# The first microseconds of an encoder step: unread bf16 products on TensorE, a norm's row factors by float32r products, and another order of weights and norms

## The chip, the cores and the metric

The kernel runs on one core of one Trainium2 chip. A core has five engines that work side by side, each with a queue of its own: TensorE (PE, matrix products into PSUM), VectorE (DVE), ScalarE (ACT), GpSimd (POOL) and SyncE (SP, which here only issues DMA transfers). An engine takes its instructions in order, and an instruction may wait on semaphores that other engines or transfers raise. The metric is the time of one execution in microseconds (us), as the median of several runs.

## The reference, cut to what matters

Two layers, each with three parts: a feed-forward block (FFN 1), a mixer with four branches, and a second feed-forward block (FFN 2). 384 frames of width 1024 go through them (256 of one new stream, 16 of each of 8 running streams). What the change touches is the very start: the first norm of FFN 1 and the first columns of its product.

```python
def rmsnorm(x, g):
    xf = x.astype(jnp.float32)
    xf = xf * lax.rsqrt(jnp.mean(jnp.square(xf), axis=-1, keepdims=True) + EPS)
    return (xf * g.astype(jnp.float32)).astype(x.dtype)

def swiglu_ffn(x, g_pre, g_post, w_gu, w_down):
    gate, up = jnp.split(rmsnorm(x, g_pre) @ w_gu, 2, axis=-1)
    return rmsnorm((jax.nn.silu(gate) * up) @ w_down, g_post)
```

## The kernel before

The 384 frames stand as three tiles of 128 frames (`x0`, `x1`, `x2`, in the code `self.x[t]`), frames on the partitions. All large products are made in float32r. Each operand is split in a high part (`wh`, `xh`: a copy cast to float32r, by ACT) and a low part (`wl`, `xl`: the rest, a subtraction by DVE), and a product is the sum of three: high by high, low by high, high by low (`mm3`).

Weights come in units of 512 KB, in the fixed order of `plan_units`. A unit is loaded by SP into one of four staging buffers (`st`), cast by ACT (`wh`) and subtracted by DVE (`wl`); only then is the staging buffer free, and SP loads the unit that stands four places later. The first four units are `ffn_gs` (here s0 to s3, called by number), 2 rows of 128 of the first 512 columns each; then `ffn_gp` and `ffn_dn` units follow.

Every norm of a tile goes through `chain`: ACT squares the two halves of the tile and sums them (`out` is a scratch tile `junk`, one buffer for all users; the sums go to `pre`), DVE adds a constant, POOL takes the power -1/2, DVE multiplies tile, factor and `gain` (SCALAR_TENSOR_TENSOR, two halves), PE transposes 4 blocks of each half (`acc<-ident,half`), ACT casts them to `xh` (two halves), DVE subtracts `xl` (two halves). `gain` is the row of 1024 norm factors on all 128 partitions. For the first norm it is made from one loaded row (`row`) by a product with a column of ones, in plain float32, and copied out of PSUM by DVE; later norms load it spread.

`ffn_head` then makes the first 512 columns for each frame tile in turn: 8 steps k of three products of 512 columns (`rot<-wh,xh`, `rot<-wl,xh`, `rot<-wh,xl`), two k per weight unit. So tile 0 needs s0 for k = 0 and 1, s1 for k = 2 and 3, s2 for k = 4 and 5, s3 for k = 6 and 7. After the three tiles `ffn_body` begins, with products of 384 columns from the `ffn_gp` units (`rot<-xh,wh` and so on).

The order in which work is written to the engines is made by a planner in Python. `self.now` is its clock; `tick` advances it by the estimated cost of each TensorE instruction, and pops queued steps (`spawn`, `yield`) that have come due, `pump` emits the next weight unit when the estimates of ACT and DVE leave room. A step with a due time (a number that is yielded, as in `chain(..., at)`) is not written before the planner's clock has reached it. So the due times of the three norms, 4000, 7000 and 10000, set where they stand among the weight casts. The estimates set the order only; on the chip each instruction starts when its engine and its semaphores let it.

The lines that matter: `run` holds the start (the row's products, the loads, the three `spawn(("xT", t), ...)`), `chain` the norms, `split_unit` the weights, `heads` the first products.

Of the kernel before, what the change touches and what calls it, by code (L numbers as in the profile page):

```python
# [8 lines left out]
F32 = mybir.dt.float32  # L9
F32R = mybir.dt.float32r  # L10
BF16 = mybir.dt.bfloat16
AF = mybir.ActivationFunctionType
ALU = mybir.AluOpType
# [3 lines left out]
P = 128  # L17
D = 1024
# [30 lines left out]
PE, ACT, DVE, POOL = "tensor", "scalar", "vector", "gpsimd"  # L49
# [50 lines left out]
class Core:  # L100
# [545 lines left out]
    def mixer_front(self, l, m, mf, ma, aT, yT):  # L646
# [201 lines left out]
        with pool("mixq") as mq:  # L848
# [48 lines left out]

            self.heads(keys, main, mid)
            run(conv(0))

            def latent_kv(t, pb):
# [98 lines left out]
            for j in range(4):  # L1000
# [6 lines left out]
                if j % 2:  # L1007
                    self.done(("uq", l, 1 + j // 2))
            run(conv(1))
            self.need(("lat",))  # L1010

# [101 lines left out]
        with pool("mixs") as ms:  # L1113
# [102 lines left out]
            for j in range(4):  # L1216
                o = self.bank()[:, :P]
                for i in range(2):
                    h = 2 * j + i
                    for k in range(2):  # L1220
                        mm(o[i * 64:(i + 1) * 64, :], lhsT=wuv[:, k, h * 64:(h + 1) * 64],
                           rhs=qa[:, k, :, h * S:(h + 1) * S], start=(k == 0), stop=(k == 1))
                self.spawn(("att",), attended(j, o), "acc")
        run(fillers)
        for f in self.idle:
            f()
# [90 lines left out]
    def run(self):  # L1317
        nc, tc, a = self.nc, self.tc, self.a
# [10 lines left out]
        with ExitStack() as es:  # L1329
# [21 lines left out]
            row = self.gains.tile([P, D], F32, tag="g", name="row")  # L1351
# [10 lines left out]

            gain = self.gains.tile([P, D], F32, tag="g", name="gain")
            es.enter_context(tc.manual_schedule(engines=ENGINES))
            one = self.half()[:, :P]
            nc.vector.memset(one[0:1], 1.0)
            for h in range(2):
                o = self.acc(2, h)
                nc.tensor.matmul(o, lhsT=one[0:1], rhs=row[0:1, h * 512:h * 512 + 512], start=True, stop=True)
                nc.vector.tensor_copy(gain[:, h * 512:h * 512 + 512], o)  # L1370
            load_x(1)
            self.arrival += 1456
            self.load_unit()
# [2 lines left out]
            self.load_unit()  # L1376
            self.load_unit()
            for t in range(NT):
                self.spawn(("xT", t), self.chain(t, None, None, gain, 4000 + 3000 * t))
            self.ffn_pool()  # L1380
            for l in range(self.depth):
                m = {}
# [153 lines left out]
```

## Time and profile before

| | us |
|---|---|
| median of 3 runs (1858.26 to 1858.51) | 1858.48 |
| the profiled execution | 1858.79 |
| its span, first to last instruction | 1857.0 |
| PE busy in the span | 1831.8 |

The profile is of one execution. Its span is 1.79 us shorter than the time of the same execution. PE is the engine to look at first: it is busy for 99% of the span. The start can be told apart by stretches: up to 8.51 us PE has only the row's products, from there to 32.88 us it makes the head of the first block, and at 32.88 us the first product of 384 columns begins.

### The profile page before, as it was taken

The numbers are of one execution on the slowest core, as the hardware profiler recorded it, in microseconds if no ns is written. First come the engines' busy times: TensorE is split into PE (matmuls) and PEld (weight loads), VectorE is DVE, ScalarE is ACT, GpSimd is POOL, SyncE is SP. The second block draws the span as 40 slices with busy tenths as digits, with TensorE's granted clock in tenths as the row PEclk, the third lists the DMA queues.
The fourth block names the chain that finished last, engine by engine and source line by source line (L and its number), as shares of the span: only waits on it lengthen the run. The fifth ranks groups of instructions, "written<-read, shape, count | busy, mean of one in ns | idle before, by whom it ended". The sixth has DMA issues, their size and how long they took to land.

```text
span 1857.0 us, 25073 instructions
## 1 busy us (share of the span) xinstructions
PE 1831.8 (99%) x10060; PEld 1704.4 (92%) x10060; DVE 952.6 (51%) x1466; ACT 699.7 (38%) x1156; POOL 47.7 (3%) x96
## 2 busy tenths in 40 slices
PE   8999999999999999999999999999999999999998
PEld 6999998889999889999989999988899998999997
DVE  5333347896544463333463333478864446533333
ACT  5333334444333443333343333445343335333332
POOL 0000001000000000000000000010000000000000
PEclk9999999999999999999999999999999999999999
DMA  7444443452343443344444434344523434443441
GB/s 252 137 125 125 125 146 94 142 178 83 114 137 124 146 159 125 125 126 126 134 137 126 128 130 129 117 102 139 173 73 127 142 123 136 148 127 126 133 125 46
DMA packets 98087, 241.88 MB, mean 130 GB/s; under 512 B 28977, under 2 KB 39985, under 8 KB 97970
## 3 DMA queue, kind: packets, MB, share of 16 engines
q1 hardware_dynamic: 97826, 240.21, 41.4%
q8 instruction: 79, 1.29, 0.3%
q14 instruction: 38, 0.31, 0.1%
q10 hardware_dynamic: 144, 0.07, 0.0%
HBM read 236.63 MB, written 3.31 MB: 129 GB/s over the span
## 4 chain that ended last, share of the span: by engine, by line
PE 93%; DVE 4%; ACT 1%; issue 1%; POOL 0%; DMA 0%; POOLq 0%; DVEq 0%; ACTq 0%
PE rot L74 59%; PE acc L74 34%; DVE yTb L74 1%; DVE wl L74 1%; DVE half L74 1%; ACT wh L74 0%; ACT junk L74 0%; DVE sv L74 0%; DVE yTd L74 0%; DVE qTp L74 0%; DVE qa L74 0%; DVE xl L74 0%; DMA st<-in_f 0%; POOL ln L74 0%; POOL kv L74 0%
## 5 line engine op out<-in xcount | busy, mean ns | idle before, releaser
L74 DVE TENSOR_TENSOR wl<-st,wh 128x1024 fp32r<-128x1024 f32 (+3 forms) x426 | 500.1, 1185 | 479.3 <-ACT wh L74 468.3
L74 ACT CAST wh<-st 128x1024 fp32r<-128x1024 f32 (+3 forms) x426 | 428.5, 1018 | 665.1 <-issue 366.3
L74 PE MATMUL rot<-xh,wh 128*128 128x384 f32 x1984 | 669.1, 337 | 0.7 <-ACT sg L74 0.7
L74 PE MATMUL rot<-xh,wl 128*128 128x384 f32 x1984 | 665.7, 336 | 0.6 <-DVE wl L74 0.6
L74 PE MATMUL rot<-xl,wh 128*128 128x384 f32 x1984 | 665.1, 335 | 0.0
L74 PEld LDWEIGHTS rot<-xh,wh 128*128 128x128 f32 x1984 | 372.5, 188 | 8.0 <-issue 3.2
L74 PEld LDWEIGHTS rot<-xh,wl 128*128 128x128 f32 x1984 | 372.6, 188 | 5.0 <-DVE wl L74 1.0
L74 PEld LDWEIGHTS rot<-xl,wh 128*128 128x128 f32 x1984 | 372.5, 188 | 0.3 <-issue 0.3
L74 PE MATMUL acc<-wl,hh 128*128 128x512 f32 x528 | 207.2, 392 | 0.0
L74 PE MATMUL acc<-wh,hl 128*128 128x512 f32 x528 | 207.1, 392 | 0.0
L74 PE MATMUL acc<-wh,hh 128*128 128x512 f32 x528 | 205.4, 389 | 0.0
L74 DVE TENSOR_TENSOR hf<-sg,rot 128x384 f32<-128x384 f32 x80 | 44.4, 555 | 146.0 <-PE rot L74 146.0
L74 PEld LDWEIGHTS acc<-wl,hh 128*128 128x128 f32 x528 | 99.1, 188 | 20.8
L74 PEld LDWEIGHTS acc<-wh,hl 128*128 128x128 f32 x528 | 99.1, 188 | 19.1
L74 PEld LDWEIGHTS acc<-wh,hh 128*128 128x128 f32 x528 | 99.2, 188 | 18.9
L74 ACT ACTIVATE half<-rot 128x384 f32<-128x384 f32 x58 | 28.5, 492 | 167.2 <-PE rot L74 167.2
L74 DVE SCALAR_TENSOR_TENSOR half<-half,acc 128x384 f32<-128x384 f32 x44 | 24.4, 554 | 124.1 <-PE acc L74 124.1
L74 DVE SCALAR_TENSOR_TENSOR yTb<-bs,cols,yTb 128x384 f32<-128x384 f32 x120 | 73.8, 615 | 2.1
L74 PE MATMUL rot<-wl,xh 128*128 128x512 f32 (+1 forms) x144 | 55.7, 387 | 1.6 <-DVE wl L74 1.6
L74 PE MATMUL rot<-wh,xh 128*128 128x512 f32 (+1 forms) x144 | 56.3, 391 | 0.0
L74 PE MATMUL acc<-ident,half 128*128 128x128 f32 x262 | 43.9, 283 | 6.7 <-DVE half L74 5.4
L74 POOL TENSOR_TENSOR post<-post,neghalf 128x1 f32<-128x1 f32 x18 | 12.2, 679 | 1440.2 <-DVE post L74 1440.0
(221 smaller groups left out, 1631.7 us busy)
## 6 DMA issues: line engine op xcount, KB each, us to landing
st<-ffn_gp SPq DMA_DIRECT2D x160, 512.0 KB, 3.5
st<-ffn_dn SPq DMA_DIRECT2D x88, 512.0 KB, 3.5
st<-in_g SPq DMA_DIRECT2D x64, 512.0 KB, 3.7
st<-in_f SPq DMA_DIRECT2D x24, 512.0 KB, 4.0
st<-ffn_gs SPq DMA_DIRECT2D x16, 512.0 KB, 4.8
st<-w_o SPq DMA_DIRECT2D x16, 512.0 KB, 4.2
st<-w_br SPq DMA_DIRECT2D x16, 384.0 KB, 3.1
st<-in_b SPq DMA_DIRECT2D x8, 512.0 KB, 4.9
```

What stands on the lines that cost most here:

```text
L74: r = f(*args, **kw)
```

## The change

Three things are done differently in `run`, before and at the first norm.

1. DVE fills the scratch tile `junk` (128 x 512, bf16) with ones, and PE multiplies it by itself 9 times into a PSUM tile that nobody reads (`idle(9)`); after the row's products it does so 11 times more (`idle(11)`). All 20 write the same PSUM buffer, `acc(1, 1)`.
2. The row is split: ACT makes a row of ones and the high part `rh` in float32r, DVE subtracts the low part `rl` (all three lie in parts of `xl` that are not in use yet), and each half of `gain` is the sum of two float32r products where it was one float32 product.
3. The planner is kept from popping work meanwhile (`self.busy`), its clock and its engine estimates are set to zero behind the products, the due times of the norms are 4000, 8200 and 12500, and `pump` is called once more.

```diff
-            one = self.half()[:, :P]
-            nc.vector.memset(one[0:1], 1.0)
+            some = self.junk(512)
+            nc.vector.memset(some, 1.0)
+            rh, rl = (self.xl[0:1, 3 * i:3 * i + 3, :].rearrange("p k t -> p (k t)")[:, :D] for i in range(2))
+            one = self.xl[0:1, 6, 0:P]
+            self.busy = True
+            def idle(n):
+                for _ in range(n):
+                    nc.tensor.matmul(self.acc(1, 1), lhsT=some[:, :P], rhs=some, start=True, stop=True)
+            idle(9)
+            nc.scalar.activation(one, self.ones[0:1], AF.Copy, scale=256.0)
+            nc.scalar.copy(rh, row[0:1])
+            nc.vector.tensor_tensor(rl, row[0:1], rh.bitcast(F32), op=ALU.subtract)
             for h in range(2):
+                sl = slice(h * 512, h * 512 + 512)
                 o = self.acc(2, h)
-                nc.tensor.matmul(o, lhsT=one[0:1], rhs=row[0:1, h * 512:h * 512 + 512], start=True, stop=True)
-                nc.vector.tensor_copy(gain[:, h * 512:h * 512 + 512], o)
+                nc.tensor.matmul(o, lhsT=one, rhs=rh[:, sl], start=True, stop=False)
+                nc.tensor.matmul(o, lhsT=one, rhs=rl[:, sl], start=False, stop=True)
+                nc.vector.tensor_copy(gain[:, sl], o)
+            idle(11)
+            self.now, self.busy = 0.0, False
+            self.free = {e: 0.0 for e in (ACT, DVE, POOL)}
...
-                self.spawn(("xT", t), self.chain(t, None, None, gain, 4000 + 3000 * t))
+                self.spawn(("xT", t), self.chain(t, None, None, gain, (4000, 8200, 12500)[t]))
+            self.pump()
```

What stands on the engines is shown at three places; words in brackets behind a row name the semaphores it waits for (an engine's name, or a transfer's DMAHW number). Behind the head, PE has the same rows in the same order before and after.

PE at the start of the program, before: the row's two products, the transposes of tile 0, the first products.

```order
L74 MATMUL acc<-row,half 128x512 [waits DMAHW1_49,DVE_49]
L74 MATMUL acc<-row,half 128x512
L74 MATMUL acc<-ident,half 128x128 [waits DMAHW0_49,DVE_49]
L74 MATMUL acc<-ident,half 128x128 x3
```

PE at the same place in the change; `junk` is the tile of ones, `xl` the split row. Of each run of unread products the first two and the last are shown.

```order
L74 LDWEIGHTS junk [waits DVE_49]
L74 MATMUL acc<-junk 128x512
L74 LDWEIGHTS junk
L74 MATMUL acc<-junk 128x512 [waits PE_49]
...
L74 MATMUL acc<-xl 128x512 [waits Activation_49]
L74 MATMUL acc<-xl 128x512 [waits DVE_49]
L74 MATMUL acc<-xl 128x512 x2
...
L74 MATMUL acc<-junk 128x512 [waits PE_49]
L74 MATMUL acc<-ident,half 128x128 [waits DMAHW0_49,DVE_49]
```

The 20 unread products stand ahead of the transposes of tile 0, and each of them but the first waits for PE's own semaphore, which is raised by the product that wrote the PSUM buffer before it.

ACT from the first norm on, before: squares of tile 0 (`x_98`), s0, squares of tile 1 (`x_99`), the casts of tile 0, s1, squares of tile 2 (`x_100`), s2.

```order
L74 ACTIVATE junk,pre<-x_98 128x512 [waits DMAHW2_49]
L74 ACTIVATE junk,pre<-x_98 128x512 [waits Activation_49]
L74 CAST wh<-st 128x1024 [waits DMAHW3_49]
L74 ACTIVATE junk,pre<-x_99 128x512 [waits DMAHW4_49,Activation_49]
L74 ACTIVATE junk,pre<-x_99 128x512 [waits Activation_49]
L74 CAST xh<-acc 128x4x128 [waits PE_49] x2
L74 CAST wh<-st 128x1024 [waits DMAHW5_49]
L74 ACTIVATE junk,pre<-x_100 128x512 [waits DMAHW6_49,Activation_49]
L74 ACTIVATE junk,pre<-x_100 128x512 [waits Activation_49]
L74 CAST wh<-st 128x1024 [waits DMAHW7_49]
```

ACT at the same place in the change.

```order
L74 ACTIVATE xl<-ones 1x128 [waits DVE_49]
L74 CAST xl<-row 1x1024 [waits DMAHW1_49]
L74 ACTIVATE junk,pre<-x_98 128x512 [waits DMAHW2_49,DVE_49,PE_49]
L74 ACTIVATE junk,pre<-x_98 128x512 [waits Activation_49]
L74 CAST wh<-st 128x1024 [waits DMAHW3_49]
L74 CAST xh<-acc 128x4x128 [waits PE_49] x2
L74 CAST wh<-st 128x1024 [waits DMAHW5_49]
L74 ACTIVATE junk,pre<-x_99 128x512 [waits DMAHW4_49,Activation_49]
L74 ACTIVATE junk,pre<-x_99 128x512 [waits Activation_49]
L74 CAST wh<-st 128x1024 [waits DMAHW7_49]
L74 CAST wh<-st 128x1024 [waits DMAHW0_49]
L74 ACTIVATE junk,pre<-x_100 128x512 [waits DMAHW6_49,Activation_49]
```

The first square has two more waits, DVE and PE: it writes the scratch tile that the unread products read. The squares of tile 1 have moved behind s1, and s2 and s3 ahead of the squares of tile 2.

DVE from tile 1's norm on, before.

```order
L74 TENSOR_SCALAR pre<-pre 128x1 [waits Activation_49]
L74 TENSOR_TENSOR xl<-acc,xh 128x4x128 [waits Activation_49]
L74 SCALAR_TENSOR_TENSOR half<-x_99,pre,gain 128x512 [waits DMAHW4_49,Pool_49]
L74 SCALAR_TENSOR_TENSOR half<-x_99,pre,gain 128x512
L74 TENSOR_TENSOR xl<-acc,xh 128x4x128 [waits Activation_49]
L74 TENSOR_TENSOR wl<-st,wh 128x1024 [waits DMAHW5_49,Activation_49]
```

DVE at the same place in the change.

```order
L74 TENSOR_TENSOR wl<-st,wh 128x1024 [waits DMAHW5_49,Activation_49]
L74 TENSOR_SCALAR pre<-pre 128x1 [waits Activation_49]
L74 SCALAR_TENSOR_TENSOR half<-x_99,pre,gain 128x512 [waits DMAHW4_49,Pool_49]
L74 SCALAR_TENSOR_TENSOR half<-x_99,pre,gain 128x512
L74 TENSOR_TENSOR wl<-st,wh 128x1024 [waits DMAHW7_49,Activation_49]
L74 TENSOR_TENSOR wl<-st,wh 128x1024 [waits DMAHW0_49,Activation_49]
```

The low part of s1 has moved ahead of tile 1's norm, and the low parts of s2 and s3 stand right behind it.

## Rows read from the trace of the kernel before

**Rows 1.** The page's first lines: span; busy time, share, instructions of PE.

```profile
span 1857.0 us, 25073 instructions
PE 1831.8 (99%) x10060; PEld 1704.4 (92%) x10060; DVE 952.6 (51%) x1466; ACT 699.7 (38%) x1156; POOL 47.7 (3%) x96
```

**Rows 2.** Stretches: from:to, length, busy per engine (instructions), granted clock, DMA share, GB/s.

```profile
0.00:8.51 8.51, 3.75 (x4) 1.16 (x5) 2.67 (x8) 4.62 (x9) 0.76 (x5) 1.00 0.76 272
8.51:14.25 5.74, 5.74 (x20) 4.54 (x20) 5.67 (x9) 4.78 (x10) 0.55 (x1) 1.00 1.01 394
14.25:32.88 18.63, 17.01 (x82) 13.79 (x82) 11.40 (x18) 9.11 (x16) 2.41 (x3) 1.00 0.69 218
32.88:140.00 107.12, 107.12 (x573) 101.14 (x571) 43.15 (x47) 36.67 (x48) 0.00 (x0) 1.00 0.44 142
```

**Rows 3.** Chain that ended last, its start: start, length, what (0 to 35 us).

```profile
2.44 3.76 PE acc L74 x4
...
6.83 0.21 DVE pre L74
...
8.51 1.98 PE acc L74 x8
...
10.52 0.03 ACT xh L74
...
18.05 1.23 DVE wl L74
...
19.32 0.97 PE rot L74 x3
20.29 0.44 PE acc L74 x4
```

**Rows 4.** Timeline, PE: start, length, operation, tiles, shapes, [idle before, releaser].

```profile
11.32 0.63 PE L74 MATMUL rot<-wh,xl 128*128 128x512 f32 x1
11.74 0.63 PE L74 MATMUL rot<-wh,xh 128*128 128x512 f32 x1
...
19.32 0.50 PE L74 MATMUL rot<-wl,xh 128*128 128x512 f32 x1 [1.62 <-DVE wl L74]
...
22.63 0.39 PE L74 MATMUL rot<-wh,xl 128*128 128x512 f32 x1
...
26.25 0.39 PE L74 MATMUL rot<-wh,xh 128*128 128x512 f32 x1
...
32.88 0.33 PE L74 MATMUL rot<-xh,wh 128*128 128x384 f32 x1
```

**Rows 5.** Timeline, DVE, ACT and POOL in the first norm.

```profile
0.86 0.17 DVE L74 MEMSET ones<- 128x128 f32 x1
0.99 0.17 DVE L74 MEMSET half<- 1x128 f32 x1
...
4.81 0.63 ACT L74 ACTIVATE junk<-x 128x512 bf16<-128x512 f32 x1 [2.38 <-DMA x<-x]
...
5.56 0.63 ACT L74 ACTIVATE junk<-x 128x512 bf16<-128x512 f32 x1
6.10 0.19 ACT L74 ACTIVATION_READ_ACCUMULATOR junk<-x 128x1 f32 x1
...
7.11 0.55 POOL L74 TENSOR_TENSOR pre<-pre,neghalf 128x1 f32<-128x1 f32 x1 [6.67 <-DVE pre L74]
```

**Rows 6.** Groups by shape, 0 to 33 us: count, busy, mean ns, idle before.

```profile
L74 DVE TENSOR_TENSOR wl<-st,wh 128x1024 fp32r<-128x1024 f32 x7 | 8.4, 1221 | 0.5 <-ACT wh L74 0.5
L74 ACT CAST wh<-st 128x1024 fp32r<-128x1024 f32 x7 | 7.2, 1045 | 0.0
...
L74 DVE SCALAR_TENSOR_TENSOR half<-x,pre,gain 128x512 f32<-128x512 f32 x6 | 4.2, 748 | 0.7 <-POOL pre L74 0.7
L74 DVE TENSOR_TENSOR xl<-acc,xh 128x512 fp32r<-128x512 f32 x6 | 4.0, 685 | 0.0
...
L74 ACT CAST xh<-acc 128x512 fp32r<-128x512 f32 x6 | 3.5, 586 | 3.5 <-PE acc L74 3.4
```

## The prediction

> **What bounds the kernel now.** I read the page's first lines, then the stretches, then the chain at the start, then single rows of PE, ACT and DVE there. PE is busy for 1831.8 of 1857.0 us [rows 1]: the sum of its products bounds the kernel, and only the 25 us in which it rests, or products that run slowly, can be given back. Behind 32.88 us it does not rest at all for 107 us (107.12 of 107.12), so what the start loses or gains is carried to the end one to one. Up to 8.51 us PE is busy for 3.75 us, and from 14.25 to 32.88 us it rests 1.6 us [rows 2]. The reader is to see three losses in the first 33 us. PE makes the row's spread in 3.76 us and then waits for the norm. From 8.51 to about 14.2 us, where the stretches are cut, it is busy throughout but slow: products of 512 columns start 0.42 us apart (11.32 to 11.74), against 0.226 us later (22.63 to 26.25, sixteen steps) [rows 4]; the first is the pace of the 1.2 GHz level, the second that of the 2.4 GHz level, though the clock column reads 1.00 for both stretches [rows 2]. And at 19.32 us PE has waited 1.62 us for a low part of weights [rows 4], which stands late on DVE. So the head is bound by PE's clock for some 5 us, and for the rest of tile 0 by the row of small steps on ACT and DVE, which the chain of waits goes through [rows 3]; then by PE.
>
> The span of the profiled run is 1857.0 us and its time 1858.79, 0.31 us over the median of 1858.48. I sum the shift of the first 384-column product, which starts at 32.88 us [rows 4], and add it to the median.
>
> **The change part by part.** Behind the head nothing moves on PE, so I follow the head.
>
> *When the first square starts (call it S).* Before, it started at 4.81 us, as soon as tile 0 had landed [rows 5]. Now it writes the scratch tile that all 20 unread products read, and it waits for PE. There is one such buffer, so the wait must be for the last of the 20. Behind the square, ACT holds everything: s0, the casts of tile 0, all later weights; DVE, POOL and PE wait through them.
>
> - First product: DVE fills the tile of ones from 0.99 us. The fill of 128x128 took 0.17 us [rows 5]; 512 elements in bf16 lie between that and four times that, so PE starts between 1.2 and 1.7 us. I take 1.3, near the row.
> - Nine products in a row, each waiting for the one before. No PE instruction in the trace waits for its own predecessor. Bounds: 0.42 us each, the distance of products that need not wait (3.8 us in all), or the full record of 0.63 us [rows 4] plus a handover of 0.03 to 0.04 us (10.49 to 10.52, 19.28 to 19.32 [rows 3]), taken as 0.05. I take 0.68 us, since a wait for the result can't end before the result: 9 x 0.68 = 6.1, to 7.4 us. That is at the lower clock; before, PE ran 3.76 us of the row's products and was slow still at 8.51 us (eight transposes in 1.98 us [rows 3], against 0.44 us for four later). I let the clock rise at about 7 us, after nearly 6 us of work, as it did between 8.51 and 14.2 us.
> - The row's split: ACT 128x1024 casts take 1.05 us and DVE's subtraction 1.22 us [rows 6]; one partition has the same length. With the row in hand at 2.44 us that ends by about 5 us, under the nine products. Costs nothing; were the nine absent it would set the start of the row's products at 5 us. It also replaces 3.76 us of float32 products by four float32r ones, 4 x 0.23 = 0.9 us at the higher clock, to 8.3 us (1.7 us at the lower).
> - Eleven products at the higher clock: record 0.39 [rows 4] plus 0.05, 11 x 0.44 = 4.8, to 13.1 us. Bounds: 11 x 0.23 = 2.5 us without waits, 11 x 0.68 = 7.5 us at the lower clock.
>
> So **S = 13.1 us**, 8.3 us later than before. Lowest: 1.3 + 9 x 0.42 + 0.9 + 2.5 + 0.2 (the last one's end) = 8.7. Highest: 1.3 + 6.1 + 1.7 + 7.5 = 16.6.
>
> *From S through tile 0, in the new order.* By then x and s0 to s3 have landed: they are issued as before, the last of them, s3, was in use at 19.32 us [rows 4], and here ACT comes to it at S+8.7, 21.8 us. So only engines count. ACT: two squares and their sums, 1.5 us (4.81 to 6.29 [rows 5]); s0 to S+2.5; casts of tile 0 behind the transposes, to S+5.0; s1 to S+6.1; tile 1's squares to S+7.6; s2 and s3 to S+9.7. DVE: the constant (0.21 [rows 3]), POOL 0.55 [rows 5] and handovers bring the first multiply to S+2.5; two of 0.75 to S+4.0; low part of s0 to S+5.2; two `xl` of 0.69 to S+6.6; low part of s1 to S+7.8; tile 1's constant and power, multiplies S+8.7 to S+10.2; low part of s2 to S+11.4 [rows 6]. That last one is what PE waits for: with k = 4. From there PE has 11 products (11 x 0.23 = 2.5) and tile 1's 8 transposes (0.9), and tile 1 begins at S+14.8. Low parts of s3 (S+12.6) come in time. The stall of 1.62 us is gone, but only because another wait, for s2, has taken its place.
>
> *Tiles 1 and 2.* 24 products at 0.226 (5.4 us), 8 transposes of tile 2 that before stood in tile 0 (0.9), 2 of the hidden block (0.2): 6.5 us. Tile 2: 5.4 + 0.2 = 5.6. First 384-column product at S + 26.9.
>
> Before: 32.88. The shift is S + 26.9 - 32.9 = **S - 6.0**: what the new order and the clock bring in is 6 minus the old S of 4.8, some 1.2 us; what S costs is 8.3 us. With S = 13.1: +7.1 us, 1858.5 + 7.1 = **1865.6 us**.
>
> *The clock in the gap.* PE rests from S to about S+3.2, when the first transposes can start. Before, after a rest of 2.3 us, the transposes ran at the lower level. If the clock falls here, the eight transposes take 2.0 instead of 0.9 us and push the casts and s1 by about 0.5 us; the products of k = 0 to 3 run low but end before s2 is ready. So 0 to +0.5 us; I take 0, as S+11.4 leaves time to rise again. The Trainium skill, in "TensorE: Matmul & The Clock Gate", section "HAM oscillation — how this bites in real kernels", says that a wait between bursts of products puts the clock back, and so speaks against warming PE ahead of a wait; the slow transposes at 8.51 us agree. By that rule the sum would be 1866.1.
>
> *Loads.* SP issues the norm row and constants ahead of some weights, and each waits for a staging buffer that DVE frees. The first `ffn_gp` load goes out when s0's low part is done, at about S+5.2; it is wanted at S+26.9. Covered by 21 us; if not, one cast and one subtraction (2.3 us) would show. The extra fill, row of ones and copies lie ahead of S: nothing.
>
> **Rivals.**
>
> *The clock does not rise during the unread products.* Then S = 16.6, plus 0.5 for low transposes: +11.1, 1869.6 us. For it: 3.76 us of the row's products did not raise it by 8.51 us, and these products wait on one another, which the slow ones of before did not. Against: PE is given work for over 11 us on end, twice the 5.7 us after which it rose before.
>
> *The unread products overlap* although each waits, because the wait is met before the drain has ended. S = 8.7 to 9.8, by when the clock rises: +2.7 to +3.8, 1861.2 to 1862.3 us. For it: products without waits start 0.226 us apart with records of 0.39 us [rows 4]. Against: the wait names PE's own semaphore. The Trainium skill, same page, section "Step-by-step: what each phase is for", says the fill of one matmul overlaps the drain of the one before, so that their distance is N cycles; by that rule alone the time would be this rival's. The trace agrees for products that don't wait and shows none that do.
>
> *Not slower: the square is held little or not at all.* If the wait on the scratch tile ends early, the norm starts when tile 0 lands, PE is at the higher clock, and only PE's own queue counts: with overlapping products the 20 end by 8.9 us, the transposes start by 9, first products at 10.2, tile 0 is set by s2's and s3's place as above, about 10.2 us long, then 12.1: 32.5, or -0.4 us: 1858.1 us. The point from which it decides is S = 6.0: below, not slower; up to S = 9.7 within 0.2%. For it: it is what the due times are written for. Against: ACT's row has the wait on PE, and one scratch buffer admits no other reading.
>
> A gain of over 0.2% (about what a measurement here can tell from no change, 3.7 us) would need both old losses, 2.0 us of slow products and 1.6 us of stall, and something more; I see nothing more.
>
> **How the numbers follow.** Forecast, 1864.9 to 1866.6 (S 12.4 to 13.7, the clock rising between 5 and 8.5 us, and its fall in the gap): 0.60. Clock stays low: 0.15. Overlap: 0.13, of which 0.10 within 0.2%. Square not held: 0.08, nearly all within 0.2%. Something unseen: 0.04, split over all. Slower by over 0.2%: 0.60 + 0.15 + 0.03 and a little less for the forecast's low end, 0.77; within 0.2%: 0.20; faster: 0.03. The range leaves out the square not held and the far ends: 1861.0 to 1869.8.
>
> **What would show it.** In the profile after: unread products 0.65 to 0.70 us apart, then 0.42 to 0.46; the first square at about 13 us, released by PE; PE at rest for some 3 us behind the last unread product; a wait for `wl` inside tile 0; the first 384-column product at about 40 us; from there the same rows as before. Wrong would be: unread products at 0.22 us apart, or a square before 9 us. If the first 384-column product is at 40 us and the time is not up by 7 us, then something later gives it back, against the full stretch [rows 2].

## The result, and the profile after

The change makes the kernel slower, by more than forecast: 1870.44 us in the median of 6 runs (1869.86 to 1872.33) against 1858.52 (1858.26 to 1859.10) for the kernel before, a ratio of 1.0063 [1.0054, 1.0073] (in brackets its 95% interval), so +11.9 us where +7.1 had been forecast. The time lies 0.6 us above the upper end of the range. The rival "the clock does not rise during the unread products" (1869.6) is the one that came true, and one more loss came with it.

The profiled run of the change took 1871.7 us. The page's first lines, as in [rows 1]:

```profile
span 1869.9 us, 25115 instructions
PE 1841.9 (99%) x10080; PEld 1704.7 (91%) x10080; DVE 955.0 (51%) x1467; ACT 700.3 (37%) x1158; POOL 46.0 (2%) x96
```

PE has 20 instructions more and is busy for 10 us more, and its share is still 99%. Such a page hides the change: PE's busy time grew, since the 20 unread products count as work for the 12.7 us of their records (5.73 and 7.01 below). Stretches tell more (from:to, length, busy per engine, granted clock, DMA share, GB/s). I cut them at the first square, at the first product of tile 0, at its longest wait, and at the first product of 384 columns:

```profile
0.00:16.33 16.33, 13.66 (x24) 3.08 (x24) 3.31 (x6) 2.53 (x3) 0.20 (x4) 1.00 0.71 261
16.33:21.32 4.99, 1.79 (x9) 1.57 (x9) 2.79 (x5) 2.96 (x6) 0.55 (x1) 1.00 0.00 0
21.32:27.96 6.64, 4.12 (x15) 2.73 (x14) 5.41 (x8) 6.11 (x12) 0.56 (x1) 1.00 0.72 262
27.96:45.39 17.43, 17.43 (x79) 14.29 (x80) 10.51 (x17) 8.09 (x14) 1.33 (x3) 0.90 0.63 180
45.39:152.51 107.12, 107.12 (x572) 101.13 (x571) 43.18 (x47) 36.66 (x48) 0.00 (x0) 1.00 0.44 138
```

The last stretch answers to the last of [rows 2], from the first 384-column product on, and as there PE is busy in all of it. So nearly the whole loss lies in the 45.39 us ahead of it, which were 32.88: a shift of 12.51 us, and the spans (1869.9 and 1857.0) differ by 12.9. The timeline of PE (start, length, operation, shapes, [idle before, releaser]) tells where:

```profile
1.63 5.73 PE L74 MATMUL acc<-junk 128*128 128x512 bf16 x9 [1.63 <-DVE junk L74]
7.29 2.07 PE L74 MATMUL acc<-xl 1*128 1x512 f32 x4
9.29 7.01 PE L74 MATMUL acc<-junk 128*128 128x512 bf16 x11
19.53 1.97 PE L74 MATMUL acc<-ident,half 128*128 128x128 f32 x8 [3.23 <-DVE half L74]
21.32 0.80 PE L74 MATMUL rot<-wh,xh 128*128 128x512 f32 x1
...
27.96 0.50 PE L74 MATMUL rot<-wl,xh 128*128 128x512 f32 x1 [1.91 <-DVE wl L74]
...
29.32 0.67 PE L74 MATMUL rot<-wh,xh 128*128 128x512 f32 x1
29.79 0.63 PE L74 MATMUL rot<-wl,xh 128*128 128x512 f32 x1
...
32.78 0.43 PE L74 MATMUL rot<-wh,xl 128*128 128x512 f32 x1
33.05 0.40 PE L74 MATMUL rot<-wh,xh 128*128 128x512 f32 x1
...
45.39 0.33 PE L74 MATMUL rot<-xh,wh 128*128 128x384 f32 x1
```

Three things stand in it. The nine and the eleven unread products have one pace, 5.73 / 9 and 7.01 / 11, both 0.64 us: nothing became faster on the way. PE then rests 3.23 us, since the norm of tile 0 has only begun. And some time behind the wait of 1.91 us inside tile 0, for the low part of s2, the products stand 0.42 to 0.47 us apart from 29.32 to 32.78 (the pace of the 1.2 GHz level) and 0.23 again from 33.05. The granted clock of that stretch is 0.90; in it, it is 1.00 from 28 to 29 us, 0.72 from 29 to 30, 0.50 from 30 to 32 and 1.00 again from 33.

The chain of waits (start, length, what) shows how one unread product hands over to the next:

```profile
2.29 0.60 PE acc L74
2.93 0.60 PE acc L74
3.57 0.60 PE acc L74
...
15.71 0.60 PE acc L74
16.33 0.73 ACT junk L74 x2
```

A record of 0.60 us and 0.04 us to the next start, from the first unread product to the last, and then ACT's square. The other engines' rows:

```profile
1.08 0.48 DVE L74 MEMSET junk<- 128x512 bf16 x1
...
3.72 1.21 DVE L74 TENSOR_TENSOR xl<-row,xl 1x1024 fp32r<-1x1024 f32 x1 [2.15 <-ACT xl L74]
...
16.33 0.63 ACT L74 ACTIVATE junk<-x 128x512 bf16<-128x512 f32 x1 [12.65 <-PE acc L74]
...
26.68 2.35 DVE L74 TENSOR_TENSOR wl<-st,wh 128x1024 fp32r<-128x1024 f32 x2
```

The square starts at 16.33 us instead of 4.81 [rows 5], released by PE after 12.65 us of rest: S = 16.33. The row was split by 4.93 us, under the nine products, as forecast.

### The profile page after: what moved, and what is told of

Same layout as the page of the kernel before. It is cut to its first block, busy times and chain, and to the rows that moved or that the text cites. A ratio compares the mean times of both kernels' runs of the same rounds, so it can differ in the third digit from the quotient of the medians.

```text
span 1869.9 us, 25115 instructions
## 1 busy us (share of the span) xinstructions
PE 1841.9 (99%) x10080; PEld 1704.7 (91%) x10080; DVE 955.0 (51%) x1467; ACT 700.3 (37%) x1158; POOL 46.0 (2%) x96
## 4 chain that ended last, share of the span: by engine, by line
PE 93%; DVE 4%; ACT 1%; issue 1%; POOL 0%; POOLq 0%; DVEq 0%; ACTq 0%
PE rot L74 59%; PE acc L74 34%; DVE yTb L74 1%; DVE wl L74 1%; DVE half L74 1%; ACT junk L74 0%; DVE sv L74 0%; DVE qTp L74 0%; ACT wh L74 0%; DVE yTd L74 0%; DVE qa L74 0%; POOL ln L74 0%; DVE sx L74 0%; ACT qTp L74 0%; DVE xl L74 0%
## 5 line engine op out<-in xcount | busy, mean ns | idle before, releaser
L74 PEld LDWEIGHTS acc<-ident,half 128*128 128x128 f32 x262 | 32.4, 143 | 18.9 <-DVE half L74 10.7
```

Of the source, the lines that this page charges most:

```text
L74: r = f(*args, **kw)
```

## The experiments

In each, "first 384-column product" is its start in the profiled run (32.88 us before, 45.39 us in the change). Diffs are against the change unless it says otherwise; ratios are against the kernel before on the same chip.

### Products that need not wait for one another

One PSUM buffer is taken once for all 20 products, so that no product has to wait for its predecessor; the square still waits for the tile of ones.

```diff
+            spare = self.acc(1, 1)
-                    nc.tensor.matmul(self.acc(1, 1), lhsT=some[:, :P], rhs=some, start=True, stop=True)
+                    nc.tensor.matmul(spare, lhsT=some[:, :P], rhs=some, start=True, stop=True)
```

> The change with one PSUM buffer taken once for all 20 unread products, so that none waits for PE's own semaphore; the first square still waits for the last of them. Theory (it is the wait of each product for the one before that kept PE at the lower level): products 0.42 us apart at first, the clock rises by about 7 us, the first square starts at 9.8 us in place of 16.3, the first 384-column product at 36.8 us, time some 1862.4 us (+3.9 over before). Rival (products of a tile of ones, or of bf16, never raise the clock): products 0.42 us apart to the end, square at 12.1 us, first 384-column product at 41.5 to 42.7 us, time 1867 to 1868.5 us.

Measured: 1864.87 us in the median of 8 (1862.74 to 1866.44), 1.003 [1.002, 1.004]; the profiled run took 1862.81. Its timeline of PE, and ACT's first square:

```profile
1.63 4.02 PE L74 MATMUL acc<-junk 128*128 128x512 bf16 x9 [1.63 <-DVE junk L74]
5.58 1.40 PE L74 MATMUL acc<-xl 1*128 1x512 f32 x4
6.91 2.55 PE L74 MATMUL acc<-junk 128*128 128x512 bf16 x11
...
9.49 0.63 ACT L74 ACTIVATE junk<-x 128x512 bf16<-128x512 f32 x1 [5.82 <-PE acc L74]
```

Nine products now take 4.02 us, and the eleven 2.55, which is 0.23 apart: the clock rose while the row's products ran. With the same operands, the same count and the same first start, it is the wait that decides. S fell from 16.33 to 9.49 and the first 384-column product to 36.84 us, 27.35 behind S. The runs fall in two groups, three from 1862.7 to 1863.0 and five from 1864.8 to 1866.4; the profile is of the first.

### A tile of ones of its own

The ones lie in another tile, which the squares don't write; the products still wait for one another.

```diff
-            some = self.junk(512)
+            some = self.half()[:, :256].bitcast(BF16)
```

> The change with the ones in a tile of their own, so that the first square does not wait for PE; the 20 products still wait for one another. Theory (PE's own queue holds the head nearly as long as the square's wait did): first square at 4.8 us, first transpose at 16.3 us behind the 20 products, first 384-column product at 42 to 43 us, time 1867.6 to 1868.5 us; the square's wait is worth 2 to 3 us only. Rival (the wait of the first square is the whole cost): time within 1 us of before, 1858 to 1859.5 us.

Measured: 1867.28 us (1865.4 to 1868.65, 5 runs), 1.0045 [1.0031, 1.0059]; first 384-column product at 41.91. Of its timeline, PE's transposes and ACT's first square:

```profile
16.09 1.91 PE L74 MATMUL acc<-ident,half 128*128 128x128 f32 x8
...
4.92 0.63 ACT L74 ACTIVATE junk<-x 128x512 bf16<-128x512 f32 x1 [1.25 <-DMA x<-x]
```

The square is free at 4.92 us, but the transposes stand behind the 20 products in PE's own queue and start at 16.09 without a rest ahead of them, instead of 19.53. So the wait of the square is worth 3.4 us by the transposes' start and 3.2 by the medians, and PE's queue holds nearly as long by itself. Both have to go.

### Both at once

The two edits above together.

```diff
-            some = self.junk(512)
+            some = self.half()[:, :256].bitcast(BF16)
+            spare = self.acc(1, 1)
-                    nc.tensor.matmul(self.acc(1, 1), lhsT=some[:, :P], rhs=some, start=True, stop=True)
+                    nc.tensor.matmul(spare, lhsT=some[:, :P], rhs=some, start=True, stop=True)
```

> Both edits: one PSUM buffer taken once and a tile of its own for the ones. Theory: first square 4.8 us, the 20 products end by about 9.7 us at the higher level, first transpose there, first 384-column product at 33.4 us, time 1859.0 us, no better than before, since the place of the weights' low parts sets tile 0. Rival (the change as meant: warm clock and no stall give back 3 us or more): time 1855 to 1856 us. If the clock stays low: first 384-column product at 39 to 41 us, 1865 to 1867 us.

Measured: 1858.55 us (1858.18 to 1860.39, 10 runs), 1.0001 [0.9992, 1.0011]. From its timeline of PE:

```profile
1.63 4.02 PE L74 MATMUL acc<-half 128*128 128x512 bf16 x9 [1.63 <-DVE half L74]
...
9.51 1.32 PE L74 MATMUL acc<-ident,half 128*128 128x128 f32 x8
...
17.29 0.50 PE L74 MATMUL rot<-wl,xh 128*128 128x512 f32 x1 [1.93 <-DVE wl L74]
```

The 12 us are gone, and nothing is won. The transposes run in 1.32 us instead of 1.98 [rows 3], but they start 1.0 us later, behind the unread products; and the faster PE waits 1.93 us for s2, which DVE has no sooner. The first 384-column product starts at 33.13 us, 0.25 later than before.

### No unread products at all

The tile of ones and both `idle` calls are left out; the split row and the new order stay.

```diff
-            idle(9)
-            idle(11)
```

> The change without the 20 unread products: split row, float32r products and new order of weights and norms alone. Theory: first square 4.8 us, first transpose 9.3 us (the split row is ready later than the float32 products were), first 384-column product at 33.6 us with the clock rising as before, time 1859.2 us. Rival (the new order alone is a loss or a gain): a clock that falls again in the wait for s2's low part gives 37.5 us and 1863 us; a gain of 1.6 us for the stall that went gives 1857 us.

Measured: 1859.0 us (1858.81 to 1860.43, 10 runs), 1.0004 [0.9994, 1.0013]; first 384-column product at 33.25. From its timeline of PE:

```profile
8.96 1.97 PE L74 MATMUL acc<-ident,half 128*128 128x128 f32 x8 [2.33 <-DVE half L74]
...
17.39 0.51 PE L74 MATMUL rot<-wl,xh 128*128 128x512 f32 x1 [1.94 <-DVE wl L74]
```

So the loss belongs to the 20 products, and none that can be measured to the row or the order. Beside the run above it also tells why a warm PE gives nothing here: slow transposes and slow first products, and yet the wait for s2 ends at 17.39, against 17.29 with the clock up. What ends last in tile 0 is the row of steps on ACT and DVE.

### The order alone

The kernel before, with the new due times only (diff against before).

```diff
-                self.spawn(("xT", t), self.chain(t, None, None, gain, 4000 + 3000 * t))
+                self.spawn(("xT", t), self.chain(t, None, None, gain, (4000, 8200, 12500)[t]))
```

> The kernel before with the new due times 4000, 8200 and 12500 alone: no unread products, the row spread by float32 products as before, squares of tile 0 at 4.8 us. Theory (the order gives back the stall for s3 and loses 0.9 us to tile 2's transposes and part of it to a new wait for s2): first 384-column product at 32.4 us, time 1858.1 us, 0.4 us under before. Rival (the order is a loss by itself, some of the 12 us of the change): 1860 us or more, with the clock falling in the wait for s2.

Measured: 1858.87 us (1858.32 to 1860.18, 11 runs), 1.0001 [0.9992, 1.001]. The first 384-column product came at 34.26, not at 32.4 as I expected. From its timeline of PE:

```profile
16.80 0.60 PE L74 MATMUL rot<-wl,xh 128*128 128x512 f32 x1 [1.75 <-DVE wl L74]
17.21 1.05 PE L74 MATMUL acc<-ident,half 128*128 128x128 f32 x4
```

Four transposes in 1.05 us, where they take 0.60 at the higher level in the other profiles: in this run the clock fell behind the wait of 1.75 us for s2 (granted clock 1.00 from 16 to 17 us, 0.53 from 17 to 18), and came back by 20.6 us. The order alone is worth nothing that can be measured.

### Half as many

Ten unread products in place of 20, still waiting for one another and holding the square.

```diff
-            idle(9)
+            idle(4)
-            idle(11)
+            idle(6)
```

> The change with 4 and 6 unread products in place of 9 and 11; all waits kept. Theory (time follows the start of the first square one to one, each waiting product costs 0.64 us): ten fewer, first square at 9.9 us in place of 16.3, first 384-column product at 37 to 39 us, time 1863 to 1865 us. Rival (a fixed cost of the waits or of the square's hold, whatever the count): 1868 us or more; second rival (the square starts as before, below 6 us): 1859 us.

Measured: 1864.41 us (1863.68 to 1866.54, 5 runs), 1.0029 [1.0017, 1.0041]. From its timeline of PE:

```profile
1.63 2.53 PE L74 MATMUL acc<-junk 128*128 128x512 bf16 x4 [1.63 <-DVE junk L74]
4.08 2.54 PE L74 MATMUL acc<-xl 1*128 1x512 f32 x4
6.56 3.81 PE L74 MATMUL acc<-junk 128*128 128x512 bf16 x6
```

The pace is 0.64 us again. Ten products fewer take 5.9 us off S (10.41): ten times 0.64, less the 0.47 by which the row's products take longer here, where they come before DVE has split the row. The median falls by 6.0 us, one to one with S, as in the prediction's shift of S less a constant.

### Half the rests

The PSUM buffer is asked for anew only ahead of every second product: only every second one waits.

```diff
-                for _ in range(n):
-                    nc.tensor.matmul(self.acc(1, 1), lhsT=some[:, :P], rhs=some, start=True, stop=True)
+                for k in range(n):
+                    if k % 2 == 0:
+                        o = self.acc(1, 1)
+                    nc.tensor.matmul(o, lhsT=some[:, :P], rhs=some, start=True, stop=True)
```

> The change with one PSUM buffer taken for each two unread products, so that only every second one waits for PE. Theory (rests between products keep the lower level): pairs 1.07 us apart. If half of the rests are enough to keep it low, square at 14.4 us, first 384-column product at 41 to 44 us, time 1867 to 1869 us. If the clock rises, as it did when no product waited, at 6 to 7 us: square at 11.6 us, first 384-column product at 38.5 us, time 1864 us. Rival (the level has nothing to do with the waits): low, as in the change.

Measured: 1865.06 us (1863.98 to 1867.89, 4 runs), 1.0035 [1.0021, 1.0048]. The profiled run is the slowest of the four, 1867.89. Its timeline of PE:

```profile
1.63 4.88 PE L74 MATMUL acc<-junk 128*128 128x512 bf16 x9 [1.63 <-DVE junk L74]
...
8.44 5.94 PE L74 MATMUL acc<-junk 128*128 128x512 bf16 x11
```

There a pair takes some 1.07 us (0.43 and 0.64) from first to last, so the clock did not rise among the unread products, S is 14.41 and the first 384-column product comes 27.50 later, at 41.91. The three others are 2.5 to 3.9 us shorter, which fits an S of 10.5 to 11.9 and a clock that rose on the way; no profile shows it, so for half the rests it stays open how often it does.

### The wait in tile 0, filled

The change, with 8 more unread products (k = 0 of tile 0 once more, into a PSUM buffer that is free) in the place where tile 0 waits for s2.

```diff
+                if first and t == 0 and k == 4:
+                    at, busy, self.busy = self.now, self.busy, True
+                    spare = self.acc(2, 1)
+                    for _ in range(8):
+                        mm(spare, lhsT=self.xh[:, 0, tt], rhs=w(0)[0], start=True, stop=True)
+                    self.now, self.busy = at, busy
```

> The change with eight more unread products (k = 0 of tile 0 once more, into a free PSUM buffer, no wait on PE) ahead of k = 4 in tile 0, that is in the 1.9 us in which PE rests there. Theory (that rest lets the clock fall, which cost 1.7 us in the profile of the change and in most of its runs): PE does not rest, products from 28 us on stay 0.23 us apart, first 384-column product at 43.7 us in place of 45.4, time 1869.3 us, and runs within 1 us of one another where the change's lie 2.5 us apart. Rival (the rest is not what lets it fall, or the eight products delay tile 0): 1870.4 us or more, same spread.

Measured: 1870.04 us (1869.82 to 1870.27, 5 runs), 1.0059 [1.0046, 1.0071]. From its timeline of PE, the fill and what follows the wait:

```profile
25.63 2.00 PE L74 MATMUL acc<-wh,xh 128*128 128x512 f32 x8
...
28.97 0.60 PE L74 MATMUL acc<-ident,half 128*128 128x128 f32 x4
29.33 0.48 PE L74 MATMUL rot<-wh,xh 128*128 128x512 f32 x1
29.64 0.39 PE L74 MATMUL rot<-wl,xh 128*128 128x512 f32 x1
29.87 0.40 PE L74 MATMUL rot<-wh,xl 128*128 128x512 f32 x1
```

S is 16.33 as in the change, the products from 29.64 stand 0.23 us apart, and the first 384-column product starts at 43.81, 1.58 us earlier than in the change's profile: there the clock fell behind the rest, and here, with work in its place, it did not. But the median came down by 0.4 us only, not by the 1.1 that I expected, while the spread of the runs fell from 2.5 to 0.45 us. Four of the change's six runs (1869.86 to 1870.58) lie near the five of this kernel, two above (1871.7, the profiled one, and 1872.33). So the clock seems to fall behind that wait in some runs of the change and not in all. Only one of the six has a profile; the mean granted clocks of the six (1.0 and 0.999 in the two shortest, 0.997 and 0.998 in the others) fit, but do not tell how often.

### The same fill without the waits between the products

The first edit and the fill together (the fill cut to its core).

```diff
+            spare = self.acc(1, 1)
-                    nc.tensor.matmul(self.acc(1, 1), lhsT=some[:, :P], rhs=some, start=True, stop=True)
+                    nc.tensor.matmul(spare, lhsT=some[:, :P], rhs=some, start=True, stop=True)
...
+                if first and t == 0 and k == 4:
...
+                    for _ in range(8):
+                        mm(spare, lhsT=self.xh[:, 0, tt], rhs=w(0)[0], start=True, stop=True)
```

> The same eight products in the kernel in which the 20 unread products overlap and the square still waits for them. Without them that kernel took 1862.74 to 1866.44 us, median 1864.87, and 1862.8 would follow from the first 384-column product of its profile (36.84 us), in which the clock did not fall. Theory: 1862.6 us, all runs within 1 us. Rival: the same spread and a median near 1864.9 us, so that something else moves it from run to run.

Measured: 1865.05 us (1862.86 to 1866.35, 7 runs), 1.0032 [1.002, 1.0043]; in the profile S is 8.70 and the first 384-column product comes at 36.35. The median and the spread are those of the first experiment. So its spread does not come from the rest in tile 0. S differs between the two profiles (9.49 and 8.70; nine products in 4.02 and 3.43 us), since the clock rose at another time; that it rises later still in other runs would explain the rest, but that is argued, not shown.

### Old due times with both edits

The kernel with both edits, and the due times of before (diff against that kernel).

```diff
-                self.spawn(("xT", t), self.chain(t, None, None, gain, (4000, 8200, 12500)[t]))
+                self.spawn(("xT", t), self.chain(t, None, None, gain, 4000 + 3000 * t))
```

> The 20 unread products overlapping and holding nothing, split row, but the due times of before (4000, 7000, 10000). Theory (at the higher clock, too, the old order has s3's low part late): first 384-column product at 34.4 us, 1.3 us behind the kernel with the new due times, time 1860 us. Rival (with the clock up the order does not matter): 33.1 us and 1858.5 us.

Measured: 1861.55 us (1859.67 to 1863.13, 10 runs), 1.0011 [1.0002, 1.002]; first 384-column product at 33.33, not 34.4. The head is as long as with the new due times: two waits of 1.36 and 1.43 us, for s1 and s3, in place of one of 1.93. The loss stands far behind it. Two stretches of this run, and then the same two of the run with both edits (columns as above):

```profile
1250.00:1270.00 20.00, 17.19 (x92) 15.00 (x91) 16.28 (x41) 8.17 (x19) 2.40 (x4) 0.91 0.41 126
1350.00:1370.00 20.00, 19.06 (x138) 16.76 (x138) 10.33 (x27) 7.01 (x16) 1.33 (x1) 0.93 0.15 47
```

```profile
1250.00:1270.00 20.00, 17.20 (x101) 15.14 (x101) 15.95 (x41) 8.50 (x18) 2.40 (x4) 1.00 0.38 125
1350.00:1370.00 20.00, 19.07 (x145) 17.13 (x144) 11.27 (x31) 6.47 (x16) 1.33 (x1) 1.00 0.15 47
```

PE rests as long in both (2.8 and 0.9 us), but in one the granted clock falls to 0.91 and 0.93. Against before, the starts of ACT's instructions stand less than 0.5 us late up to 1290 us, 1.06 from 1310 and 2.60 from 1376. So the loss of the profiled run, which lies near the median, arises in the mixer with the falls of the clock there, and not in the head. For the other runs that is not shown: two of the ten have a mean granted clock of 1.0 and took 1859.67 and 1861.14 us. Whether the due times have a part in it is open.

### A fill of the first rest only

Before's row in plain float32, with 1 unread product ahead of it and 6 behind it, which wait for nothing and end as tile 0's norm does (diff against before, shortened).

```diff
+            some = self.half()[:, :256].bitcast(BF16)
+            nc.vector.memset(some, 1.0)
+            spare = self.acc(1, 1)
...
+            idle(1)
...
+            idle(6)
...
-                self.spawn(("xT", t), self.chain(t, None, None, gain, 4000 + 3000 * t))
+                self.spawn(("xT", t), self.chain(t, None, None, gain, (4000, 7000, 12500)[t]))
```

> The kernel before with its float32 row products, seven unread products that wait for nothing and hold nothing (own tile, one PSUM buffer), one ahead of the row's products and six in the rest behind them, and due times 4000, 7000 and 12500. Theory: clock high from the transposes at 8.5 us on, squares at 4.8 us, s2's low part earlier; first 384-column product at 31.2 us, 1.7 us earlier than before, time 1856.8 us. Rival (the six products stand in front of the transposes and delay them, or the clock does not rise): 1858 to 1859.5 us.

Measured: 1858.53 us (1857.73 to 1860.01, 11 runs), 0.9998 [0.9989, 1.0007]. The head is the shortest of all; the first 384-column product comes at 31.62, 1.26 us ahead of before. From its timeline of PE:

```profile
6.10 2.74 PE L74 MATMUL acc<-half 128*128 128x512 bf16 x6
8.64 1.92 PE L74 MATMUL acc<-ident,half 128*128 128x128 f32 x8
...
14.23 0.50 PE L74 MATMUL rot<-wl,xh 128*128 128x512 f32 x1 [1.26 <-DVE wl L74]
```

The unread products end where the transposes begin. But the eight transposes take 1.92 us, against 1.32 in the run with both edits, and the first two products start 0.41 us apart; 0.23 apart they stand from 11.44 only. I had expected the higher level from the transposes on. PE had worked since 1.76 us without a rest, for 3.78 us of it on the row's float32 products: having no rests was not enough here. And the profiled run gives the gain back: 0.9 us around 650 us, with a wait of 0.6 us for a norm that before does not have, and 0.5 us at about 1300 us, behind this stretch (columns as above), in which the clock fell:

```profile
1250.00:1270.00 20.00, 17.21 (x94) 15.18 (x93) 15.70 (x39) 8.45 (x18) 2.40 (x4) 0.91 0.41 125
```

In the median no gain is left that can be measured.

### Both edits and the fill

The kernel with both edits, and the 8 products in tile 0's wait.

```diff
-            some = self.junk(512)
+            some = self.half()[:, :256].bitcast(BF16)
+            spare = self.acc(1, 1)
-                    nc.tensor.matmul(self.acc(1, 1), lhsT=some[:, :P], rhs=some, start=True, stop=True)
+                    nc.tensor.matmul(spare, lhsT=some[:, :P], rhs=some, start=True, stop=True)
...
+                if first and t == 0 and k == 4:
...
+                    for _ in range(8):
+                        mm(spare, lhsT=self.xh[:, 0, tt], rhs=w(0)[0], start=True, stop=True)
```

> The 20 unread products overlapping and holding nothing, new due times, and the eight products in the rest of tile 0. Theory: the rest is the wait for s2's low part, which does not move, so the first 384-column product stays at 33.1 to 33.3 us; only the runs in which the clock fell get better: time 1858.4 us, within 0.5 us of one another. Rival (the warm start pays once nothing lets the clock fall): 1857 us or less.

Measured: 1858.77 us (1858.34 to 1862.04, 11 runs), 1.0002 [0.9993, 1.001]; first 384-column product at 32.94. Nothing won, and the spread is no smaller. No version tried beats the kernel before.

## Why the prediction was right and where it was wrong

**What bounds the kernel: right.** Behind the head PE is as full as before, and what the head lost reached the end: 12.51 us at its end, 12.9 in the span. Half as many products gave half the loss back.

**The square waits for the last unread product: right,** and so are the two small steps under cover (the row's split, the loads). The run with a tile of its own adds what the forecast's argument had left out: PE's queue alone holds the transposes to 16.09 us.

**S: mis-sized, 16.33 for 13.1, the largest part of the miss.** Term by term, as the prediction summed it:

| | forecast | measured |
|---|---|---|
| first product starts | 1.3 | 1.63 |
| nine products | 6.1 | 5.66 |
| row's four products | 0.9 | 2.00 |
| eleven products | 4.8 | 7.04 |
| S | 13.1 | 16.33 |

The failed step is the sentence "I let the clock rise at about 7 us, after nearly 6 us of work, as it did between 8.51 and 14.2 us". The products of before to which it points need not wait, and start 0.42 us apart with no rest [rows 4]; these wait for their predecessor's end and start 0.64 us apart, half as much again as 0.42. In that state TensorE stayed at the lower level for all 14.7 us, and it did again in the profiles of the three other kernels with such waits between all products (own tile and filled wait with 20 of them, half as many with 10). Where the wait was taken away and nothing else, it rose after 4 to 5 us. Why rests of this kind keep it low no run shows. I had the evidence "against" of that rival on the wrong footing: "given work for over 11 us on end" is not what the queue shows when each product waits.

The Trainium skill, in "TensorE: Matmul & The Clock Gate", section "A second HAM failure mode: psum-queue depth-cycling", tells of a kernel that cycles through PSUM banks, where tiny rests of TensorE between groups of products make the clock swing between its levels. The trace differs: here one buffer is asked for anew per product, and during the unread products the clock does not swing, it does not rise. The same page, section "Single matmul latency", gives (219 + N)/1.2 ns for a product by itself at the lower level, 609 ns for 512 columns as an estimate; the records of 0.60 us agree, and the 0.04 us of handover come on top.

The smaller terms: the fill of 128x512 in bf16 took 0.48 us, so that PE started at 1.63, near the upper of my two bounds (1.2 and 1.7), where I had chosen one near the lower; and a waiting product took 0.64 us, since its record is 0.60, not 0.63, with 0.04 of handover. A guess of 0.68 was close.

**From S to the first 384-column product: order right, size 0.5 to 0.8 us short, and 2.2 in the change's own profile.** The forecast was 26.9 us. Five other profiles, in which the square was held too and the clock did not fall inside tile 0, give 27.35 (products without waits), 27.45 (half as many), 27.50 (pairs), 27.48 (filled wait) and 27.65 (the same fill without the waits). In the filled wait 0.2 us of it lie ahead of s2's low part and some 0.4 behind it. The wait for s2 came as named, at S + 11.6 for 11.4, and it took the place of the old stall. The transposes ran at the lower level, as feared, and that costs little.

**The clock in the gap: I took 0 and looked at the wrong gap.** The gap behind S was weighed; the one inside tile 0, which I had found myself as the wait for s2, was not. In the profiled run the clock fell behind it: 17.43 us from there to the first 384-column product, against 15.85 with the rest filled. The section of the Trainium skill that the prediction set against the change, "HAM oscillation — how this bites in real kernels" of the same page, is borne out in kind, though the waits that it tells of, some 3 to 5 us, are longer than the 1.91 us here. The filled wait agrees (no fall in its profile, and little spread), but it does not show that the rest alone is the cause: five other profiles have the same rest and no fall behind it. By the runs' spread it happens in some executions of the change, not in all, so it is worth 1.6 us in the profile and perhaps 0.4 to 0.6 in the median.

**The sum.** Of the 4.8 us that the median lies above the forecast, 3.2 are S and 0.6 the path behind it. The 1.0 left is 0.4 by the fall in tile 0 (the filled wait's median against the change's; 0.6 if each is first set against the median of before measured with it, 1858.52 and 1858.71) and 0.6 that the filled wait's median lies above what its head gives (1858.48 + 10.93): 0.2 of it arises behind the head (spans of 1868.1 and 1857.0), 0.3 is that the profiled run of before lies above its median, and 0.2 that this kernel's lies below.

**The rival "not slower": its condition was not met, and its price was near.** With both waits gone the kernel takes 1858.55 us, where 1858.1 had been named. The reason stands in the wait for s2: it ends at 17.29 us with the clock up and at 17.39 without any unread products, so that a faster PE only comes to it sooner.

**The range.** It ended at 1869.8, 0.2 above the rival "clock stays low". Its S of 16.6 was near (16.33), its 0.5 us for low transposes too; what it lacked is the fall of the clock in tile 0 and the 0.6 us. A rival's own spread belongs in the range, not only its middle.

## What to carry to other kernels

Work that is put in to bring TensorE's clock up must not wait for itself, nor hold others: one PSUM buffer taken once, not asked for anew per product, and an operand tile that nobody else writes. Ask of each idle wait in the new order, not only of the one that the change aims at, whether the clock can fall behind it. And before TensorE is warmed, look at what ends last behind it: where that is a row of steps on ACT and DVE, as here, a faster PE only waits for it, and the gain is nothing.

## What the runs showed of the hardware

- Products of 128x512 in bf16 that each wait for the one before start 0.64 us apart (record 0.60) and left the clock at the lower level for 14.7 us; the same products without the wait started 0.42 us apart, and it rose after 4 to 5 us (in the filled kernel, by the nine products' 3.43 us, after some 3), to 0.23 apart. With float32 products of the row among them it had not risen 8 us after PE's first start, though PE did not rest (the fill of the first rest).
- The same rest may or may not be followed by a fall of the clock: waits of 1.75 to 1.92 us for s2 were followed by one in the profiles of the change, of the tile of its own and of the order alone, and waits of 1.92 to 1.94 us were not in those of the products without waits, of both edits, of no unread products, of half the count and of pairs. Where it fell, it did so with PE at work again: in the change that wait ended at 27.96 us, and the granted clock is 1.00 from 28 to 29 us and 0.50 from 30.
- In the mixer, over 1200 us on, rests of the same length cost nothing in the profile of both edits, and 0.6 and 1.5 us in that with the old due times, where the granted clock fell to 0.91 and 0.93. Some of the scatter of single runs by 1 to 2 us may be this; that is not shown.
- The column of the granted clock reads 1.00 through the first 16 us of the change, though the pace there is that of the lower level: records of 0.60 us against 0.39 later, and without the waits starts 0.42 us apart, as the products stand between 30 and 32 us of the change, where the column reads 0.50. So at the start of this program the pace of the products tells the clock, not the column.
